# Weight splits of the first mixer ahead in ScalarE's and VectorE's order, and cumulative gate sums in two products

## The chip, the cores and the metric

The kernel runs on one core of one Trainium2 chip. TensorE (PE in the profile) does the matrix products, VectorE (DVE) and ScalarE (ACT) the elementwise work, GpSimd (POOL) some small elementwise work, and SyncE (SP) issues most of the DMAs. Each engine takes its instructions in the order in which they stand in its own queue, and waits by semaphores for what other engines or DMAs have to deliver. The metric is the device time of one execution in microseconds (us); of several executions the median counts.

## The reference

One inference step of a trunk of two layers, for a prompt of 512 tokens and 8 samples of 8 tokens (64 rows), with a model width of 1024. Layer 0 is a forgetting attention in parallel with a gated linear recurrence; layer 1 is a pooling mixer; each is followed by a convolutional feed-forward part. The change touches the first mixer only. Cut to that:

```
def _mixer_ab(xn, past, h0, conv_prev, p, li):
    proj = jnp.einsum("btd,de->bte", xn, p["ab_w_in"][li])
    q, k, v, f, xr, gate = jnp.split(proj, IN_SPLITS, axis=-1)
    q = _rmsnorm(q..., p["ab_q_gain"][li])
    k = _rmsnorm(k..., p["ab_k_gain"][li])
    logf = jax.nn.log_sigmoid(f + p["ab_b_f"][li])
    ...
    c_all = jnp.cumsum(lf_all, axis=1)
    attn = _fox_attention(q, k_all, v_all, c_all[:, past_len:], c_all, ...)
    xc, conv_new = _causal_dwconv(xr, conv_prev, ...)
    h, h_last = _rglru(xc, h0, ...)
    y_rg = h * jax.nn.gelu(gate)
    merged = jnp.concatenate([attn, y_rg], axis=-1)
    out = jnp.einsum("bte,ed->btd", merged, p["ab_w_out"][li])
```

Everything is float32. `logf` has 8 heads; the prompt's 512 tokens lie as 4 chunks of 128 on the partitions, so `cumsum` over tokens is a sum within a chunk plus the totals of the chunks ahead of it.

## The kernel before

The activations stand transposed, features on the partitions, with all 576 tokens in the free dimension. A product in full precision is made of three products in a faster format: each weight and each activation is split into a high part (a cast) and the remainder as low part, and `mm3` (L124 to L137) sums high by high, high by low and low by high, in two column halves of 288 tokens, each into a bank of PSUM. There are 8 banks. `proj_tok` (L550 to L573) does the same with tokens on the output's partitions, four chunks and one bank for the samples.

The weights come from HBM through `raw` (L106 to L111, tile `wraw`, two buffers, DMAs issued by SP). `split` (L112 to L122) makes the high half with a copy on ScalarE (L119) and the low half with a subtraction on VectorE (L120), into the tile `whl`, which has two buffers. So a split can be made at most two ahead of PE's use, and a third waits until PE has read the first.

The order of the instructions on each engine is set by a scheduler when the kernel is built: it takes what is ready by its priority, which follows from the place in the program, unless an instruction is pinned to the program's order or stands in a block that has a high priority. `load_x` is such a block: it transposes x with PE (L346, L347), casts it (L352, L353, and L366, L367 for the samples), and holds the pinned split for the first product `proj(0)` at chunk 5. Its weights, and those of `proj(1)`, lie in one tile, raw0, whose halves are loaded by two DMAs (L329 and L335).

The parts of the mixer, in the program's order: `proj(0)`, the gate product `forget` (L494), the loading and transposing of parameters (`params`: L204 casts the page table into the tile `more`, L206 and L208 transpose parameters), `proj(1)`, then the recurrence's convolutions and gates, the projection of k with `proj_tok`, `branch(0)` (the gate's product, with `gt` L1470), `qk_norm` for k (L595, L596 on ScalarE, L597 to L605 on VectorE), `branch(1)`, the transposes of k (L625 splits, L631 transposes, L633 copies to kT), the recurrence's scan (L1421 to L1433), the projection of q, `branch(2)`, `branch(3)`, the projection of v with background work between its steps, and the output projection `out_proj` over the recurrent half with the evacuation of v (L461 to L463) beside it. In that background stand `sums` (L523 to L538), which makes the prompt's cumulative sums of logf with ten products of 128x8, and `rows` (L545), which transposes them. Attention follows, then the other half of `out_proj`.

Of the kernel before, what the change touches and what calls it, by code (L numbers as in the profile page):

```python
# [2 lines left out]

# [5 lines left out]
F32 = mybir.dt.float32  # L9
# [7 lines left out]
MUL, ADD, SUB = ALU.mult, ALU.add, ALU.subtract  # L17

P = 128
# [7 lines left out]
H = 8  # L27
# [16 lines left out]
class Trunk:  # L44
    def __init__(self, tc, ctx, I, O):
        self.tc, self.nc, self.ctx, self.I, self.O = tc, tc.nc, ctx, I, O
        self.pool = lambda name, **kw: ctx.enter_context(tc.tile_pool(name=name, **kw))
        self.const = self.pool("const", bufs=1)
        self.res = self.pool("res", bufs=1)
        self.wr = self.pool("wr", bufs=2)  # L50
        self.wh = self.pool("wh", bufs=2)
        self.sm = self.pool("sm", bufs=2)
        self.mm = self.pool("mm", bufs=8, space=PSUM)

        self.mid, self.pre, self.bg = deque(), deque(), deque()
        self.up0 = None


    def tick(self):
# [53 lines left out]
    def split(self, v, k, n, pin=False):  # L113

        t = self.wh.tile([P, 2, 1024], F32R, name="whl", tag="whl")
        hi = t[:, 0, 0:k * n].rearrange("p (k n) -> p k n", k=k)
        lo = t[:, 1, 0:k * n].rearrange("p (k n) -> p k n", k=k)
        keep = self.tc.keep_in_program_order if pin else (lambda ins: ins)
        keep(self.nc.scalar.copy(hi, v))  # L119
        keep(self.nc.vector.tensor_tensor(lo, v, hi.bitcast(F32), SUB))  # L120
        return hi, lo

    def mm3(self, whi, wlo, xs, K, first=0):
# [264 lines left out]
    def mixer_ab(self):  # L388
        nc, I, O, tc = self.nc, self.I, self.O, self.tc
        V, A, G, PE = nc.vector, nc.scalar, nc.gpsimd, nc.tensor  # L390
        w_in = I["ab_w_in"][0].rearrange("(k p) n -> p k n", p=P)
        with tc.tile_pool(name="mix", bufs=1, reuse_waits="tile") as mp, ExitStack() as att:
            lf = mp.tile([P, 5, H], F32, name="lf")
# [4 lines left out]
            qn = mp.tile([P, 4, NS], F32, name="qn")  # L398
            kn = mp.tile([P, 4, NS], F32, name="kn")
            bg = self.bg  # L400
            with tc.tile_pool(name="yy", bufs=1, reuse_waits="tile") as yp:
                with tc.tile_pool(name="rg", bufs=1, reuse_waits="tile") as rp:
                    self.tokp = rp
# [73 lines left out]
                self.out_proj(lambda k: (yh[:, k, :], yl[:, k, :]), 4, range(8), prepare)  # L477
            self.attention(mp, aq, q2s, zs, kT, cq, ck, vh, vl, qn, kn, vs, lf, ds, ah, al)
            att.close()
            self.new_xg(1)  # L480
            self.out_proj(lambda k: (ah[:, k, :], al[:, k, :]), 0, (4, 5, 6, 7, 0, 1, 2, 3),
                          lambda m: self.xg_chunk(m, self.g_ffn(0, m)))
# [15 lines left out]
    def gates(self, mp, pf, lf, cq, ck):  # L498


        nc, O = self.nc, self.O
        V, A, G, PE = nc.vector, nc.scalar, nc.gpsimd, nc.tensor
        fT = self.res.tile([16, T], F32, name="fT", tag="sqacc", bufs=1)
        for hf in range(2):
            A.copy(fT[:, hf * HT:(hf + 1) * HT], pf[hf][0:16, 0:HT])

        def logf():
            ft = self.bank()
            for i in range(6):
                a, b, r = (i * P, i * P + P, 0) if i < 4 else (NP, T, (i - 4) * NS)  # L510
                j = min(i, 4) * 16
                PE.matmul(ft[r:r + b - a, j:j + 16], fT[:, a:b], self.ident[0:16, 0:16], start=True, stop=True)
            fsb = self.sm.tile([P, 5, 2, H], F32, name="fsb", tag="fsb", bufs=1)
            A.copy(fsb, ft[:, 0:80].rearrange("p (i a h) -> p i a h", i=5, a=2))
            z = self.sm.tile([P, 5, H], F32, name="z", tag="rs", bufs=1)
            V.tensor_tensor(z, fsb[:, :, 0, :], fsb[:, :, 1, :], ADD)
            V.tensor_tensor(z, z, self.rt.unsqueeze(2).to_broadcast([P, 5, H]), MUL)
            V.tensor_tensor(z, z, self.rowb[:, 128:136].unsqueeze(1).to_broadcast([P, 5, H]), ADD)
            self.logsigmoid(lf.rearrange("p i h -> p (i h)"), z.rearrange("p i h -> p (i h)"), [P, 40], "40")
            nc.sync.dma_start(O["logf_p"][0, 0].rearrange("(i p) h -> p i h", p=P), lf[:, 0:4, :])  # L520
            nc.sync.dma_start(O["logf_s"][0].rearrange("b t h -> (b t) h"), lf[0:NS, 4, :])

        def sums():  # L523
            ct = self.ct = mp.tile([P, 2, 4, 2, 4, 32], F32, name="ct", tag="X")
            pc = self.bank()
            for i in range(4):
                for j in range(i + 1):
                    PE.matmul(pc[:, i * H:(i + 1) * H], self.triu if j == i else self.ones, lf[:, j, :],
                              start=(j == 0), stop=(j == i))
            chi = self.sm.tile([P, 32], F32R, name="chi", tag="chi", bufs=1)  # L530
            V.tensor_copy(chi, pc[:, 0:32])
            G.memset(ct, 0.0)
            G.memset(ct[:, 0, :, :, :, 0:2], 1.0)
            G.memset(ct[:, 1, :, :, :, 2:4], 1.0)
            v4 = lambda t: t.rearrange("p (i t j) -> p i t j", i=4, t=2)
            V.tensor_copy(ct[:, 0, :, :, :, 2], v4(chi.bitcast(F32)))
            V.tensor_tensor(ct[:, 0, :, :, :, 3], v4(pc[:, 0:32]), v4(chi.bitcast(F32)), SUB)
            G.tensor_scalar(ct[:, 1, :, :, :, 0:2], ct[:, 0, :, :, :, 2:4], -1.0, None, MUL)  # L538

        def rows():  # L540
            for a, dst in ((0, cq), (1, ck)):
                for t in range(2):
                    ps = self.bank()
                    for i in range(4):
                        PE.transpose(ps[:, i * P:(i + 1) * P], self.ct[:, a, i, t].rearrange("p j r -> p (j r)"), self.ident)  # L545
                    A.copy(dst[:, t, :], ps)

        self.bg.append(logf)
        return [sums, rows]

    def proj_tok(self, w_in, c0):
# [64 lines left out]
    def k_prep(self, mp, kT):  # L616

        V, A, PE, X = self.nc.vector, self.nc.scalar, self.nc.tensor, self.X
        x2 = mp.tile([P, 2, H, 2, DH], F32R, name="x2", tag="Xq")

        def split(i):
            x = X[:, i, :].rearrange("p (h d) -> p h d", h=H)
            hi, lo = x2[:, i % 2, :, 0, :], x2[:, i % 2, :, 1, :]
            A.copy(hi, x)
            V.tensor_tensor(lo, x, hi.bitcast(F32), SUB)  # L625

        def step(i):
            for a in range(2):
                pt = self.bank()
                for h in range(4):  # L630
                    PE.transpose(pt[:, h * P:(h + 1) * P],  # L631
                                 x2[:, i % 2, 4 * a + h].rearrange("p s d -> p (s d)").bitcast(F32), self.ident)
                (V.tensor_copy if a else A.copy)(kT[:, 4 * a:4 * a + 4, i * P:(i + 1) * P],  # L633
                                                 pt.rearrange("p (h t) -> p h t", h=4))
            if i < 2:
                split(i + 2)

        split(0)
        split(1)
        return [lambda i=i: step(i) for i in range(4)]  # L640
# [878 lines left out]
```

## Time and profile before

| | us |
|---|---|
| median of 3 runs | 1306.14 (1304.78 to 1307.19) |
| the profiled execution | 1310.66 |
| its span | 1308.9 |
| PE busy | 1288.2 (98%) |
| VectorE busy | 813.9 (62%) |
| ScalarE busy | 532.8 (41%) |
| POOL busy | 167.4 (13%) |
| high halves, L119, 176 of them | 183.1 (1.041 each) |
| low halves, L120, 176 of them | 214.7 (1.220 each) |

The span runs from the first to the last instruction; the 1.8 us between it and the execution's own time lie around it. PE is busy nearly throughout, and 20.7 us of the span are not. Busy time says nothing of the pace: PE's clock has two levels, and the page's row of the granted clock, or the windows, show in which of them it worked. The first mixer has 28 of the 176 splits, of which 23 stand ahead of the end of attention and are not pinned; ends of PE's rows are modelled, so a distance between the starts of two rows says more than a duration.

### The profile page before, as it was taken

Reading aid. Unit: us, or ns where it says so; the run is one execution under the profiler, and the core shown is the slowest. Engines: PE = TensorE matmul, PEld = TensorE weight load, DVE = VectorE, ACT = ScalarE, POOL = GpSimd, SP = SyncE. Lnnn points to the kernel's source line nnn. Section 1 sums busy time; section 2 is a strip of 40 time slices with the busy share of each in tenths; the row PEclk is TensorE's granted clock in tenths of the full one; section 3 lists DMA queues with packets and bytes.
Section 4 is the critical chain, followed back from the end, with each engine's and each line's share of the span. In section 5 each row is a group of like instructions: output and inputs, shape, how many; then the busy total and the mean of one; then the engine's idle time right before and its main releaser. Section 6 shows DMA issues by size and latency. Waiting matters only on the chain.

```text
span 1308.9 us, 23023 instructions
## 1 busy us (share of the span) xinstructions
PE 1288.2 (98%) x9462; PEld 1233.3 (94%) x9462; DVE 813.9 (62%) x1559; ACT 532.8 (41%) x877; POOL 167.4 (13%) x527
## 2 busy tenths in 40 slices
PE   8999999999999999999999999999999999999998
PEld 6987888779999999999999999899999999999998
DVE  6847847887767635765367657776743666346742
ACT  6656445674433313332133335444321343124421
POOL 2240053446100000000000002210000000000000
PEclk9999999999999999999999999899999999999999
DMA  6223232424233132312321212232223222223121
GB/s 175 85 67 101 78 130 81 122 60 130 71 100 105 38 97 97 99 65 68 110 83 36 66 50 82 84 131 66 68 67 129 65 82 70 79 97 99 34 92 49
DMA packets 105918, 111.64 MB, mean 85 GB/s; under 512 B 6722, under 2 KB 96970, under 8 KB 105805
## 3 DMA queue, kind: packets, MB, share of 16 engines
q1 hardware_dynamic: 101668, 101.68, 24.2%
q0 software_dynamic: 3072, 8.46, 2.3%
q8 instruction: 74, 1.21, 0.4%
q14 instruction: 32, 0.25, 0.1%
q10 hardware_dynamic: 1072, 0.04, 0.1%
HBM read 104.14 MB, written 6.25 MB: 84 GB/s over the span
## 4 chain that ended last, share of the span: by engine, by line
PE 90%; DVE 5%; ACT 3%; issue 1%; DMA 0%; ACTq 0%
PE mmb L132 77%; PE mmb L564 4%; PE mmb L856 2%; DVE whl L120 1%; PE mmb L821 1%; PE mmb L346 1%; PE mmb L807 1%; DVE xl L282 0%; ACT zh L1098 0%; ACT whl L119 0%; DVE xl L463 0%; PE mmb L494 0%; PE mmb L570 0%; DVE xT L1128 0%; ACT eb L794 0%
## 5 line engine op out<-in xcount | busy, mean ns | idle before, releaser
L132 PE MATMUL mmb<-xh,whl 128*128 128x288 f32 x3456 | 616.5, 298 | 3.3 <-DVE whl L120 1.7
L132 PEld LDWEIGHTS mmb<-xh,whl 128*128 128x128 f32 x3456 | 513.9, 190 | 7.0 <-DVE whl L120 2.2
L132 PE MATMUL mmb<-xl,whl 128*128 128x288 f32 x1728 | 372.6, 297 | 1.6 <-DVE xl L282 1.6
L119 ACT CAST whl<-wraw 128x1024 fp32r<-128x1024 f32 (+1 forms) x176 | 183.1, 1041 | 374.0 <-PE mmb L132 271.6
L132 PEld LDWEIGHTS mmb<-xl,whl 128*128 128x128 f32 x1728 | 280.1, 190 | 2.1 <-DVE xl L282 2.1
L132 PE MATMUL mmb<-hh,whl 128*128 128x288 f32 x1536 | 271.2, 297 | 0.1
L120 DVE TENSOR_TENSOR whl<-wraw,whl 128x1024 fp32r<-128x1024 f32 (+1 forms) x176 | 214.7, 1220 | 79.6 <-ACT whl L119 74.2
L132 PEld LDWEIGHTS mmb<-hh,whl 128*128 128x128 f32 x1536 | 226.2, 188 | 0.7 <-ACT hh L1237 0.6
L132 PE MATMUL mmb<-hl,whl 128*128 128x288 f32 x768 | 165.0, 296 | 0.0
L658 DVE TENSOR_TENSOR xT<-mmb,xT 128x288 f32<-128x288 f32 x128 | 52.6, 452 | 158.9 <-PE mmb L132 158.6
L1217 DVE TENSOR_TENSOR u<-mmb,rb 128x288 f32<-128x288 f32 x96 | 44.0, 458 | 135.4 <-PE mmb L132 127.4
L1222 POOL COPY ut<-u 128x18 f32<-128x18 f32 x96 | 23.1, 241 | 782.3 <-DVE u L1219 782.3
L132 PEld LDWEIGHTS mmb<-hl,whl 128*128 128x128 f32 x768 | 123.1, 188 | 0.0
L1237 ACT CAST hh<-hf 128x576 fp32r<-128x576 f32 x48 | 32.3, 674 | 139.0 <-DVE hf L1234 139.0
L1226 ACT ACTIVATE t<-u,par 128x592 f32<-128x592 f32 x96 | 84.6, 881 | 3.6 <-POOL u L1221 2.0
L1228 DVE SCALAR_TENSOR_TENSOR t<-u,par,t 128x592 f32<-128x592 f32 x96 | 80.1, 835 | 3.4
L1227 DVE SCALAR_TENSOR_TENSOR t<-u,par,t 128x592 f32<-128x592 f32 x96 | 79.6, 830 | 1.1 <-ACT t L1226 1.0
L1231 ACT ACTIVATE t<-t 128x592 f32<-128x592 f32 x48 | 33.6, 699 | 95.0 <-DVE t L1228 95.0
L1238 DVE TENSOR_TENSOR hl<-hf,hh 128x576 fp32r<-128x576 f32 x48 | 36.4, 759 | 34.8 <-ACT hh L1237 34.8
L564 PE MATMUL mmb<-whl,xh 128*128 128x512 f32 x192 | 53.7, 400 | 0.0
L564 PEld LDWEIGHTS mmb<-whl,xh 128*128 128x128 f32 x192 | 35.9, 191 | 8.2
L1218 DVE TENSOR_TENSOR u<-mmb,rb 128x224 f32<-128x224 f32 x96 | 36.6, 382 | 0.0
(383 smaller groups left out, 1311.4 us busy)
## 6 DMA issues: line engine op xcount, KB each, us to landing
wraw<-in_ffn_w_up SPq DMA_DIRECT2D x48, 1024.0 KB
wraw<-in_ffn_w_down SPq DMA_DIRECT2D x24, 1024.0 KB
wraw<-in_ab_w_in SPq DMA_DIRECT2D x9, 1024.0 KB
wraw<-in_ab_w_out SPq DMA_DIRECT2D x4, 1024.0 KB
xt<-in_x_prompt SPq DMA_DIRECT2D x4, 512.0 KB
out_y_p<-y SPq DMA_DIRECT2D x8, 256.0 KB
wraw<-in_ab_w_in SPq DMA_DIRECT2D x2, 512.0 KB
out_k_p<-X SPq DMA_DIRECT2D x1, 1024.0 KB
```

The source lines that it names most:

```text
L119: keep(self.nc.scalar.copy(hi, v))
L120: keep(self.nc.vector.tensor_tensor(lo, v, hi.bitcast(F32), SUB))
L132: nc.tensor.matmul(ps[hf][:, 0:HT], w[:, k, :], x[:, hf * HT:(hf + 1) * HT], start=(n == 0 and j == 0), stop=(n == K - 1 and j == 2))
L564: PE.matmul(ps[i], x[:, i * P:(i + 1) * P], w[:, k2, :], start=(k == 0 and j == 0), stop=(k == 7 and j == 2))
L658: self.nc.vector.tensor_tensor(x, ps[hf][:, 0:HT], x, ADD)
L1217: V.tensor_tensor(u[:, 2:2 + HT], ps[0][:, 0:HT], self.rb[:, 0:HT], MUL)
L1218: V.tensor_tensor(u[:, 2 + HT:514], ps[1][:, 0:NP - HT], self.rb[:, HT:NP], MUL)
L1226: A.activation(t, u[:, 2:594], AF.Identity, scale=self.fw(l, 2, ch), bias=self.fb(l, ch))
L1227: V.scalar_tensor_tensor(t, u[:, 1:593], self.fw(l, 1, ch), t, MUL, ADD)
L1228: V.scalar_tensor_tensor(t, u[:, 0:592], self.fw(l, 0, ch), t, MUL, ADD)
L1231: A.activation(tg[:, 0:592], tg[:, 0:592], AF.Gelu_apprx_tanh)
L1238: V.tensor_tensor(hl, hf_, hh.bitcast(F32), SUB)
```

## The change

A flag `eager` is set when the mixer's body begins, and taken back when attention is done. While it is set, a split that is not pinned is issued in a block of high priority, so that its two instructions go ahead of others that are ready on ScalarE and VectorE. And `sums` forms prefix sums of the chunks on POOL (`pre`) and then needs two products in place of ten: the triangle by all four chunks at once (32 columns), and the ones by the prefixes (24 columns), summed in the same bank.

```
@@ split
-        keep(self.nc.scalar.copy(hi, v))
-        keep(self.nc.vector.tensor_tensor(lo, v, hi.bitcast(F32), SUB))
+        with self.tc.high_priority() if self.eager and not pin else nullcontext():
+            keep(self.nc.scalar.copy(hi, v))
+            keep(self.nc.vector.tensor_tensor(lo, v, hi.bitcast(F32), SUB))
@@ mixer_ab
             bg = self.bg
+            self.eager = True
...
             att.close()
+            self.eager = False
@@ sums
+            pre = self.sm.tile([P, 3, H], F32, name="pre", tag="pre", bufs=1)
+            G.tensor_copy(pre[:, 0], lf[:, 0, :])
+            for i in range(1, 3):
+                G.tensor_tensor(pre[:, i], pre[:, i - 1], lf[:, i, :], ADD)
...
-            for i in range(4):
-                for j in range(i + 1):
-                    PE.matmul(pc[:, i * H:(i + 1) * H], self.triu if j == i else self.ones, lf[:, j, :],
-                              start=(j == 0), stop=(j == i))
+            PE.matmul(pc[:, 0:32], self.triu, lf[:, 0:4, :].rearrange("p i h -> p (i h)"), start=True, stop=False,
+                      skip_group_check=True)
+            PE.matmul(pc[:, 8:32], self.ones, pre.rearrange("p i h -> p (i h)"), start=False, stop=True,
+                      skip_group_check=True)
```

The added lines move the numbers of those behind them by 2, 3, 4, 5 or 10: L119 and L120 become L122 and L123, L204 becomes L207, L1428 becomes L1438.

What stands on VectorE at the start, between the samples' casts of the first half of x (L366, L367) and the cast of the page table (L204). `whl_185` is the split of `proj(0)`. Before:

```order
L367 SCALAR_TENSOR_TENSOR xl_75<-xT_73,gm_78,xh_74 128x64 x2
L353 SCALAR_TENSOR_TENSOR xl_77<-mmb_170,gm_78,xh_76 128x512
L354 COPY xT_73<-mmb_170 128x512
L120 TENSOR_TENSOR whl_185<-wraw_91,whl_185 128x1024
L353 SCALAR_TENSOR_TENSOR xl_77<-mmb_179,gm_78,xh_76 128x512
L353 SCALAR_TENSOR_TENSOR xl_77<-mmb_191,gm_78,xh_76 128x512
```

And now, with `whl_418`, the split of `proj(1)`:

```order
L370 SCALAR_TENSOR_TENSOR xl_75<-xT_73,gm_78,xh_74 128x64
L123 TENSOR_TENSOR whl_418<-wraw_91,whl_418 128x1024
L370 SCALAR_TENSOR_TENSOR xl_75<-xT_73,gm_78,xh_74 128x64
L356 SCALAR_TENSOR_TENSOR xl_77<-mmb_170,gm_78,xh_76 128x512
L357 COPY xT_73<-mmb_170 128x512
L123 TENSOR_TENSOR whl_185<-wraw_91,whl_185 128x1024
L356 SCALAR_TENSOR_TENSOR xl_77<-mmb_179,gm_78,xh_76 128x512
```

The second split's low half moved from far behind (it stood after the first norm's statistics) to ahead of the first split's own. On ScalarE its high half stands directly behind that of `whl_185`, ahead of the copy and casts of chunks 3 and 5 to 7.

VectorE around the recurrence's scans (L1428), where `branch(2)` begins on PE. `whl_1395` and `whl_1457` are the two splits that follow the projection of k. Before:

```order
L1428 SCALAR_TENSOR_TENSOR sq_260<-a__257,xc_258 128x512 x2
L120 TENSOR_TENSOR whl_1395<-wraw_1393,whl_1395 128x1024
L1432 TENSOR_TENSOR sq_260<-a__257,stT_261 128x4x8
L633 CAST kT_245<-mmb_1387 128x4x128
L1433 TENSOR_TENSOR sq_260<-sq_260,xc_258 128x4x8
L120 TENSOR_TENSOR whl_1457<-wraw_1393,whl_1457 128x1024
```

Now, from the last of the scans on (the first three stand ahead of these rows, and `whl_1395` ahead of them all):

```order
L1438 SCALAR_TENSOR_TENSOR sq_260<-a__257,xc_258 128x512
L123 TENSOR_TENSOR whl_1457<-wraw_1393,whl_1457 128x1024
L1438 SCALAR_TENSOR_TENSOR sq_260<-a__257,xc_258 128x512
L643 CAST kT_245<-mmb_1387 128x4x128
L1442 TENSOR_TENSOR sq_260<-a__257,stT_261 128x4x8
```

Both splits moved ahead of scans that they stood behind.

VectorE in the output projection, with L463 for the low part of v, L658 (now L668) for the sums into xT and L725 (now L735) for a part of attention's queries. Before:

```order
L463 TENSOR_TENSOR xl_1829<-vt_1830,xh_1828 128x512
L725 CAST z_1845<-mmb_1846 64x256
L725 CAST z_1854<-mmb_1855 64x256
L120 TENSOR_TENSOR whl_1932<-wraw_1871,whl_1932 128x1024
L658 TENSOR_TENSOR xT_73<-mmb_1904,xT_73 128x288
```

Now (the tile is `whl_1928`):

```order
L123 TENSOR_TENSOR whl_1928<-wraw_1867,whl_1928 128x1024
L732 COPY z_1841<-cq_246 4x128 x2
L732 COPY z_1850<-cq_246 4x128 x2
L467 TENSOR_TENSOR xl_1825<-vt_1826,xh_1824 128x512 x2
L668 TENSOR_TENSOR xT_73<-mmb_1872,xT_73 128x288
```

The low half moved ahead of all four L463 (L467 now).

## Rows read from the trace of the kernel before

**Rows 1.** What PE waited for: us in total, times, longest.

```profile
PE mmb L132 <- DVE whl L120: 3.5, 3, 1.7
...
PE mmb L132 <- ACT whl L119: 0.9, 1, 0.9
...
PE mmb L132 <- ACT kT L633: 0.5, 1, 0.5
```

**Rows 2.** What SP's queue waited for, in the first 120 us.

```profile
SPq L180 <- DMA wraw<-in_ab_w_in: 1.1, 1, 1.1
```

**Rows 3.** Timeline of SP's queue: start, us, instruction.

```profile
13.97 0.22 SPq L180 DMA_DIRECT2D more<-in_ab_q_gain  x1
```

**Rows 4.** Timeline of ScalarE at the start: start, us, instruction, count.

```profile
12.39 1.04 ACT L119 CAST whl<-wraw 128x1024 fp32r<-128x1024 f32 x1
```

**Rows 5.** Timeline of VectorE at the start.

```profile
12.89 0.63 DVE L367 SCALAR_TENSOR_TENSOR xl<-xT,gm,xh 128x64 fp32r<-128x64 f32 x2
13.44 0.74 DVE L353 SCALAR_TENSOR_TENSOR xl<-mmb,gm,xh 128x512 fp32r<-128x512 f32 x1
...
14.70 1.21 DVE L120 TENSOR_TENSOR whl<-wraw,whl 128x1024 fp32r<-128x1024 f32 x1
...
19.99 0.15 DVE L204 CAST more<-more 1x16 f32<-1x16 int32 x1
```

**Rows 6.** Timeline of PE at the start.

```profile
20.35 0.27 PE L206 MATMUL mmb<-ident,more 56*128 56x56 f32 x1
```

**Rows 7.** Timeline of ScalarE at branch(1).

```profile
90.70 1.05 ACT L119 CAST whl<-wraw 128x1024 fp32r<-128x1024 f32 x1
```

**Rows 8.** Timeline of PE at branch(1) and the k heads; in brackets idle time before, releaser.

```profile
91.80 0.53 PE L132 MATMUL mmb<-xh,whl 128*128 128x288 f32 x2 [0.88 <-ACT whl L119]
...
93.15 0.79 PE L132 MATMUL mmb<-xh,whl 128*128 128x288 f32 x4 [0.56 <-DVE whl L120]
...
105.55 1.03 PE L631 MATMUL mmb<-ident,x 128*128 128x128 f32 x8
```

**Rows 9.** Timeline of VectorE at the k heads.

```profile
103.83 1.28 DVE L625 TENSOR_TENSOR x<-X,x 128x512 fp32r<-128x512 f32 x2
```

**Rows 10.** Timeline of VectorE at branch(2).

```profile
129.80 1.20 DVE L120 TENSOR_TENSOR whl<-wraw,whl 128x1024 fp32r<-128x1024 f32 x1
```

**Rows 11.** Timeline of PE at branch(2).

```profile
128.34 0.38 PE L132 MATMUL mmb<-xh,whl 128*128 128x288 f32 x1
...
131.05 1.25 PE L132 MATMUL mmb<-xh,whl 128*128 128x288 f32 x4 [1.19 <-DVE whl L120]
...
135.07 0.69 PE L132 MATMUL mmb<-xh,whl 128*128 128x288 f32 x4
...
135.87 0.70 PE L132 MATMUL mmb<-xh,whl 128*128 128x288 f32 x4
```

**Rows 12.** Timeline of PE at the sums.

```profile
166.19 0.39 PE L528 MATMUL mmb<-lf,triu 128*128 128x8 f32 x2
...
168.45 1.83 PE L564 MATMUL mmb<-whl,xh 128*128 128x512 f32 x4
...
173.34 1.09 PE L564 MATMUL mmb<-whl,xh 128*128 128x512 f32 x4
...
176.57 2.19 PE L545 MATMUL mmb<-ident,ct 128*128 128x128 f32 x16
```

**Rows 13.** Timeline of VectorE at the output projection.

```profile
181.88 4.35 DVE L463 TENSOR_TENSOR xl<-vt,xh 128x512 fp32r<-128x512 f32 x3 [0.64 <-ACT vt L462]
```

**Rows 14.** Timeline of PE at the output projection.

```profile
189.82 0.81 PE L132 MATMUL mmb<-yh,whl 128*128 128x288 f32 x4 [1.72 <-DVE whl L120]
```

**Rows 15.** Windows at branch(2): us, busy by engine, PE's granted clock, DMA share, GB/s.

```profile
130.00:131.00 1.00, 0.00 (x0) 0.00 (x0) 1.00 (x2) 1.00 (x3) 0.98 (x1) 1.00 0.00 0
...
132.00:133.00 1.00, 1.00 (x6) 1.00 (x5) 1.00 (x2) 0.77 (x2) 0.00 (x0) 0.50 0.00 0
```

**Rows 16.** Window behind the sums, columns as in rows 15.

```profile
170.00:171.00 1.00, 1.00 (x4) 0.73 (x3) 0.32 (x1) 0.00 (x0) 0.83 (x2) 0.50 0.03 8
```

More of the change, by code (lines that the diff above doesn't have):

```diff
@@ L1 @@
 from collections import deque
-from contextlib import ExitStack
+from contextlib import ExitStack, nullcontext
 import concourse.bass as bass
@@ L479, in mixer_ab @@
             att.close()
+            self.eager = False
             self.new_xg(1)
```

## The prediction

> **What bounds the kernel now.** I read the table of engines first: TensorE (PE) is busy 98% of the span, so only what PE waits for, or what it executes itself, can move the time. Then the list of PE's waits: in the first mixer it waits three times for the low half of a split weight (VectorE, L120), once for the high half (ScalarE, L119) and once for a kT copy, 4.9 us in all [rows 1]. Outside the start these are all the gaps that the change can close. Then the timelines of ScalarE, VectorE and PE around each gap, to see what the late split stood behind, and last the granted clock in windows of 1 us, since two stretches of the mixer run at half speed. In these stretches PE is not idle in the list and yet loses time. The dumps of the instruction order say what stands where afterwards; all durations are those of the trace.
>
> **The change part by part.** Times are of the profiled execution (1310.66 us, of which the span is 1308.9); a minus is a gain.
>
> *Start, a new wait.* The kernel before does the split for `proj(0)` alone and goes on with the casts of x. Now the split for `proj(1)` (whl_418) stands directly behind it on ScalarE, and its low half stands on VectorE between the two L367 of the first sample half, ahead of the rest of x's preparation. Its raw weights are the second half of raw0. SP's issue of the q gain was held for that transfer [rows 2] and ran at 13.97 [rows 3], so they landed just before 13.97. ScalarE finishes the first split at about 13.4 [rows 4] and now sits until 13.97; the second high half takes 1.04, so it is ready at 15.0. VectorE's low half of 1.21 follows, to 16.2, then the second L367 (half of 0.63), and L353 of chunk 4, which started at 13.44, starts at about 16.4: +3.0 [rows 5]. From there to L204 VectorE has no gap in the trace (20.14 less 13.44 is all work), so L204, the cast of the page table, ends at 23.1 and not at 20.14. PE's L206, a transpose of the tile that L204 writes, follows L204 at once, at 20.35 [rows 6], and everything of PE stands behind it; now it comes at about 23.3. The L494 products ahead of it need no x that is later than they are. After this PE is gapless for 70 us, so the shift stays: **+3.0**. The bounds: +1.1 if only the L120 itself counts (the raw weights are there before ScalarE is free), +4.1 if the transfer lands a further split later. I take the row's 13.97.
>
> *branch(1).* The high half stood behind ten norm activations and ran at 90.70 [rows 7]; PE waited 0.88 for it and 0.56 for the low half [rows 8]. Now it stands behind the first two of the ten, some 4 us earlier, and both waits go. What is late next: in the k norm the low half of the following split now stands ahead of two of the L605, one L120 earlier in VectorE's queue, and with ScalarE's norm activations 0.95 later L625 (103.83, half of a pair) [rows 9] would end at about 105.5 instead of 104.5. PE, freed of 1.44 and of the late starts on either side (about 0.3), and with two L564 now ahead of the L631 that needs it (0.46), would come to that L631 at 104.3 instead of 105.55 and wait 1.2 for it. Of 1.7 some 0.5 is left: **−0.5**, between 0 and −1.7.
>
> *branch(2).* The low half ran at 129.80 behind four scans and four multiplies [rows 10]; now it stands ahead of the first scan, and is done 4 us before PE asks. PE starts this product at 128.34 and gets going at 131.05, four matmuls later; at full pace six take 0.80 (from 135.07 to 135.87), so four take 0.54 [rows 11]. The kT bank wait of 0.5 within it is covered too, as PE now does six matmuls of the other column half first, which is 0.8 us. 2.71 less 0.54 and a remainder of 0.15: **−2.0**; if only the idle part for L120 goes, −1.2.
>
> *Sums.* Ten products are 20 passes, from 166.19 to 168.45: 0.113 each. Two products are four. A pass of 32 columns is not in the trace; between the 8-column pass at 0.113 and the 128-column pass of L545 (2.19 / 16 = 0.137) [rows 12] four cost 0.45 to 0.55: **−1.8**. POOL's copy and two adds come some 100 us ahead of the use, when POOL is idle, and cost nothing; uncovered, they would be under 1 us.
>
> *out_proj.* The low half stood behind three L463 of 4.35 us in all [rows 13] and PE waited 1.72 [rows 14]. Now both halves precede L463. ScalarE's evacuations of ct and v come one split (0.95) later; a bank wait of 0 to 0.5 may follow: **−1.5**, between −1.2 and −1.8.
>
> Other splits of the mixer move as well, and SP's weight loads with them, one of them ahead of the writes of logf. PE's list has no wait for any of these weights after the start, so there is nothing to gain; its lead of several us is what hides them. A loss there would be one split, 1.2.
>
> Sum without clock: 3.0 − 0.5 − 2.0 − 1.8 − 1.5 = **−2.8**.
>
> *Clock.* Behind the window at 130, in which PE is idle, the granted clock is 0.50, that is 1.2 of 2.4 GHz [rows 15]: the 18 L132 from 131.05 to 135.07 take 4.02, where 18 at full pace take 2.4: 1.6 lost [rows 11]. Behind the twenty narrow passes it is 0.50 at 170 [rows 16]: the L564 block from 168.45 to 173.34 takes 4.89, the next, alike, 3.23 to 176.57 [rows 12]: 1.7 lost. Both causes shrink (no gap; four passes in place of twenty), so −3.3 more. Against it stands the new gap at the start. It is 3 us long, where the one at branch(2) was followed by the fall, and those of 1.44 (0.88 and 0.56) [rows 8] and 1.72 [rows 14] were followed by work at full pace. A fall there costs what it cost at 131: +1.6. The three together: −2.8 − 3.3 + 1.6 = **−4.5**.
> The Trainium skill ("TensorE: Matmul & The Clock Gate", Part 1: The HAM clock gate) says that an idle array falls back to 1.2 GHz and regains 2.4 only after being kept busy, which speaks against this change: by it the longest gap, at the start, is the first to be paid for. By that rule alone the sum would be −4.5, without it −6.1; the trace agrees at branch(2) and does not at branch(1) and the output projection.
>
> **How this stands to the median.** The profiled execution is 4.5 us above the median of 1306.14. I carry over the difference, not the level: 1306.14 − 4.5 = 1301.6.
>
> **The rivals.**
> *The clock is not gained.* The half-speed stretches may belong to this one execution (it is 4.5 us slower than the median, and they are worth 3.3), or may come again after four passes as after twenty. For it speaks that gap, against it that both fall on spots that every execution has. Then −2.8, or −1.2 with a fall at the start: 1303.3 to 1304.9.
> *No wait at the start.* If the second half of raw0 is there when ScalarE gets to it and L204's lateness is met by other slack of PE, the term of +3.0 goes: −5.8 without the clock, −9.1 with it: 1297.0 to 1300.3. Against it: the transfer's row is plain.
> *The start decides: slower.* The place is ScalarE's and VectorE's queues at 13 us. The price is the upper bound of 4.1, and a half-speed spell behind a gap of that length that lasts twice as long as the one at 131 and loses 3.3: 7.4. With the other terms at their lower ends (0 at branch(1), 1.2, 1.7 and 1.2: 4.1) and no clock back, the time is 3.3 over the median: 1309.4. It decides from a start of 6.7 (4.1 + 2.6). For it speaks that on VectorE everything up to L204 stands behind the blocked low half; against it that both dearer halves have to come together.
> *Moved, not gained.* The gaps at branch(1), branch(2) and out_proj close, but the next waits of the same chains take their place, as at the L631. Only the sums stay: 3.0 − 1.8 − about 1: 1306 to 1307. What speaks for it is branch(1); against it that at branch(2) nothing waits behind the split but small scans.
>
> **How the numbers follow.** Forecast 0.45, with 1299.5 to 1303.5 as its own range; clock not gained 0.20; no wait at the start 0.12; start decides 0.12; moved 0.11. A measurement of this kernel tells some 0.2%, 2.6 us, from no change, that is outside 1303.5 to 1308.8. Faster: 0.42 + 0.05 + 0.12 = 0.59. Same: 0.03 + 0.15 + 0.09 + 0.02 = 0.29. Slower: 0.10 + 0.02 = 0.12. The range 1298.0 to 1307.5 leaves out the lower half of "no wait" and most of "start decides", under 0.2.
>
> **What would show it.** In the profile after: PE's list with a wait of about 3 us for L204 (now L207) and none of over 0.5 for the mixer's L119 and L120 (now L122, L123); ScalarE idle for half a us between two splits at 13.5; a wait of PE at the transposes of the first k heads near 105; four passes in place of twenty, with the clock at 1.00 behind them; and the clock at 1.00 where `branch(2)` begins. A start without the wait, or a clock of 0.50 that stays behind the sums, would make the forecast wrong.

## The result

The kernel after takes 1296.39 us (median of 4 runs, 1295.60 to 1297.09), the kernel before 1306.42 (1304.78 to 1307.19): a ratio of 0.9923 [0.9911, 0.9936], 10.0 us less. The forecast was 1301.6 with a range of 1298.0 to 1307.5. The sign was right; the gain, 0.8%, is more than twice the forecast 4.5, and the time lies below the range. The profiled execution of after took 1295.6 us (span 1293.9, granted clock 0.997).

PE's list of waits in the kernel after: of what stood in [rows 1] nothing is left, and one short bank wait is new.

```profile
PE mmb L343 <- DMA gr<-in_norm_mix: 3.5, 1, 3.5
PE mmb L349 <- DMA xt<-in_x_prompt: 1.7, 1, 1.7
PE mmb L817 <- DVE st L805: 1.4, 1, 1.4
PE mmb L135 <- DVE xl L285: 1.1, 2, 0.8
...
PE mmb L555 <- DVE both L588: 0.3, 1, 0.3
```

The wait that the forecast put at the start is missing: no L209 and nothing on L207.

**Start.** ScalarE's timeline after, start, us and instruction (answers to [rows 4]):

```profile
14.08 1.05 ACT L122 CAST whl<-wraw 128x1024 fp32r<-128x1024 f32 x1 [0.47 <-DMA wraw<-in_ab_w_in]
```

VectorE's (to [rows 5]):

```profile
15.16 1.23 DVE L123 TENSOR_TENSOR whl<-wraw,whl 128x1024 fp32r<-128x1024 f32 x1 [1.80 <-ACT whl L122]
16.50 0.74 DVE L356 SCALAR_TENSOR_TENSOR xl<-mmb,gm,xh 128x512 fp32r<-128x512 f32 x1
...
23.05 0.15 DVE L207 CAST more<-more 1x16 f32<-1x16 int32 x1
```

PE's (to [rows 6]):

```profile
21.27 0.27 PE L209 MATMUL mmb<-ident,more 56*128 56x56 f32 x1
...
29.50 0.52 PE L214 MATMUL mmb<-more,ones 1*128 1x152 f32 x2
```

Up to VectorE all came as worked out: ScalarE sits 0.47 for the raw weights, chunk 4 starts at 16.50 (forecast 16.4), the cast of the page table ends at 23.20 (forecast 23.1). But PE's transpose L209 runs at 21.27, ahead of that cast. It does not wait for it.

**branch(1) and the k heads.** ScalarE, VectorE and PE after (to [rows 7 to 9]):

```profile
85.46 1.04 ACT L122 CAST whl<-wraw 128x1024 fp32r<-128x1024 f32 x1
```
```profile
104.33 1.27 DVE L635 TENSOR_TENSOR x<-X,x 128x512 fp32r<-128x512 f32 x2
```
```profile
104.44 0.63 PE L574 MATMUL mmb<-whl,xh 128*128 128x512 f32 x2
105.06 1.09 PE L641 MATMUL mmb<-ident,x 128*128 128x128 f32 x8
```

Both waits are gone. The wait of 1.2 that was to come behind the first k heads is not in the list.

**branch(2).** VectorE, PE and the window behind it, after (to [rows 10, 11, 15]); a window's columns are us, busy share of PE, PEld, VectorE, ScalarE and POOL, granted clock, DMA share, GB/s:

```profile
123.19 1.22 DVE L123 TENSOR_TENSOR whl<-wraw,whl 128x1024 fp32r<-128x1024 f32 x1
```
```profile
127.31 0.38 PE L135 MATMUL mmb<-xh,whl 128*128 128x288 f32 x1
127.65 0.43 PE L135 MATMUL mmb<-xh,whl 128*128 128x288 f32 x2
```
```profile
130.00:131.00 1.00, 1.00 (x10) 1.00 (x9) 1.00 (x2) 1.00 (x2) 0.00 (x0) 1.00 0.00 0
```

The low half is done 3 us before PE asks; no gap, and no spell at 1.2 GHz behind it.

**Sums and output projection.** PE after, and the window behind the sums (to [rows 12, 14, 16]):

```profile
161.52 0.41 PE L536 MATMUL mmb<-lf,triu 128*128 128x32 f32 x2
161.77 0.38 PE L538 MATMUL mmb<-pre,ones 128*128 128x24 f32 x2
161.99 1.18 PE L574 MATMUL mmb<-whl,xh 128*128 128x512 f32 x4
...
170.22 0.63 PE L555 MATMUL mmb<-ident,ct 128*128 128x128 f32 x4 [0.28 <-DVE both L588]
...
179.98 0.69 PE L135 MATMUL mmb<-yh,whl 128*128 128x288 f32 x4
180.51 0.42 PE L135 MATMUL mmb<-yl,whl 128*128 128x288 f32 x2
```
```profile
163.00:164.00 1.00, 1.00 (x6) 0.83 (x5) 0.88 (x1) 0.00 (x0) 1.00 (x1) 1.00 0.00 0
```

Four passes take 161.52 to 161.99, 0.47; the clock stays at 1.00 behind them. The product that waited 1.72 follows without a gap.

**Where the time went, by stages of PE.** Each stage runs from the start of one marked instruction in PE's timeline to the start of the next (us). The first mark is the transpose L206 (L209 after); what lies ahead of it is not in the table, and it starts at 20.35, 20.98, 21.27 and 19.99 us in the four profiles. Two profiles of each kernel, since a second one of before, taken with the experiments (1305.9 us, span 1304.2), differs from the first in four stages although the program is the same.

| stage | before | before, again | after | after, again |
|---|---|---|---|---|
| L206 to the end of the k projection | 63.79 | 63.81 | 63.74 | 63.79 |
| branch(1) | 17.95 | 16.48 | 16.00 | 15.99 |
| q projection | 25.23 | 25.22 | 25.28 | 25.28 |
| branch(2) | 11.30 | 9.77 | 7.79 | 7.79 |
| next products | 27.18 | 27.18 | 27.05 | 27.06 |
| sums and the block behind | 10.77 | 10.74 | 7.34 | 7.33 |
| up to q's transposes | 3.99 | 3.99 | 4.19 | 4.19 |
| output projection | 28.03 | 28.03 | 25.68 | 25.88 |
| attention | 118.61 | 117.77 | 116.53 | 116.55 |
| the rest | 977.22 | 975.70 | 974.44 | 974.53 |

Between the two middle profiles, which lie nearest to the medians (before again, after): 0.5 at branch(1), 2.0 at branch(2), 3.4 at the sums, 2.15 at the output projection (2.35 less the 0.20 of the new bank wait ahead of it; 1.95 by the second profile of after), and 1.2 each in the attention and the rest, where the order did not change.

### The profile page after: what moved, and what is told of

It reads as the page before. It is cut to its first block, busy times and chain, and to the rows that moved or that the text cites. A ratio compares the mean times of both kernels' runs of the same rounds, so it can differ in the third digit from the quotient of the medians.

```text
span 1293.9 us, 23002 instructions
## 1 busy us (share of the span) xinstructions
PE 1278.9 (99%) x9446; PEld 1226.2 (95%) x9446; DVE 813.7 (63%) x1559; ACT 532.0 (41%) x877; POOL 168.5 (13%) x530
## 4 chain that ended last, share of the span: by engine, by line
PE 94%; DVE 3%; ACT 2%; issue 1%; DMA 0%; ACTq 0%
PE mmb L135 78%; PE mmb L574 5%; PE mmb L866 2%; PE mmb L1098 1%; PE mmb L831 1%; PE mmb L349 1%; PE mmb L817 0%; DVE xl L285 0%; PE mmb L499 0%; PE mmb L580 0%; PE mmb L578 0%; DVE whl L123 0%; PE mmb L883 0%; DMA xt<-in_x_prompt 0%; PE mmb L1191 0%
## 5 line engine op out<-in xcount | busy, mean ns | idle before, releaser
L122 ACT CAST whl<-wraw 128x1024 fp32r<-128x1024 f32 (+1 forms) x176 | 182.9, 1040 | 369.9 <-PE mmb L135 269.7
L123 DVE TENSOR_TENSOR whl<-wraw,whl 128x1024 fp32r<-128x1024 f32 (+1 forms) x176 | 214.6, 1220 | 82.5 <-ACT whl L122 82.1
L668 DVE TENSOR_TENSOR xT<-mmb,xT 128x288 f32<-128x288 f32 x128 | 52.6, 452 | 157.0 <-PE mmb L135 156.8
L1232 POOL COPY ut<-u 128x18 f32<-128x18 f32 x96 | 23.1, 241 | 776.4 <-DVE u L1229 776.4
L574 PE MATMUL mmb<-whl,xh 128*128 128x512 f32 x192 | 53.2, 394 | 0.0
L574 PEld LDWEIGHTS mmb<-whl,xh 128*128 128x128 f32 x192 | 35.4, 188 | 8.1 <-ACT a__257 L1421 0.3
```

What stands on the lines that cost most here:

```text
L574: PE.matmul(ps[i], x[:, i * P:(i + 1) * P], w[:, k2, :], start=(k == 0 and j == 0), stop=(k == 7 and j == 2))
L668: self.nc.vector.tensor_tensor(x, ps[hf][:, 0:HT], x, ADD)
```

## The experiments

**1. Is there a wait at the start?** Theory A (the forecast): L206 needs what L204 writes, and the delay of VectorE costs 3 us. Theory B: it needs something else, and the delay costs nothing. First the kernel before with priority for that one split alone:

```diff
+                    self.eager = True
                     rg.proj(1)
+                    self.eager = False
```

> The kernel before, with the high priority for the split of proj(1) alone. Theory A (L206 never waited for L204, whose row only stood beside it): VectorE is 3 us late at the start and PE does not see it; 1306.4, between -0.5 and +1. Theory B (the prediction: PE's L206 waits for L204): PE waits 3 us and the kernel takes 1309.4. Theory C (the late start of the full clock seen in the changed kernel comes from this move): +0.9, 1307.3, with L494 at half pace until 20.3 us.

Then the kernel after without that split's priority:

```diff
-            self.eager = True
...
                     rg.proj(1)
+                    self.eager = True
```

> The changed kernel, with the split of proj(1) back at its ordinary place (the flag is set after proj(1)). Theory A (the early split at the start costs nothing): the same as the changed kernel, 1296.4 within 1. Theory B (it costs what it adds to VectorE): 3 us less, 1293.4. Theory C (it costs a later start of the full clock): 0.9 less, 1295.5.

Measured: 0.9996 [0.9985, 1.0007] and 0.9922 [0.9906, 0.9938] to before; the kernel after has 0.9923. So no cost of the start is to be seen, with the rest of the change or without it: alone it is a gain of 0.5 us, between a loss of 0.9 and a gain of 2.0, and a loss of 3 lies outside. VectorE and PE of the first kernel:

```profile
15.50 1.23 DVE L123 TENSOR_TENSOR whl<-wraw,whl 128x1024 fp32r<-128x1024 f32 x1 [2.23 <-ACT whl L122]
...
23.39 0.15 DVE L207 CAST more<-more 1x16 f32<-1x16 int32 x1
```
```profile
20.90 0.27 PE L209 MATMUL mmb<-ident,more 56*128 56x56 f32 x1
```

The cast is 3.4 us later than in [rows 5], the transpose only 0.55 later than in [rows 6], and 2.5 ahead of the cast. The code says why: L207 writes `more[0:1, 264:280]`, L209 reads `more[0:56, 0:P]`, columns 0 to 127. Same tile, other columns, no dependence. The reader of the cast is L214, which reads `more[0:1, 128:280]` and runs at 29.50 in the kernel after, 6.3 us behind the cast's end. That is the cover. The 0.55 is not the split's either: over all thirteen profiles this instruction starts anywhere from 18.50 to 23.09, on average at 21.18 in the five with the split ahead and at 21.12 in the eight without. In all five it starts ahead of the cast, by 1.7 to 4.2 us. VectorE's lateness does reach PE in one of them, the second profile of after, in which PE's clock was at 2.4 GHz from 13 us on and PE came to the L494 products (L499 there) early:

```profile
18.47 0.30 PE L499 MATMUL mmb<-xl,wf 128*16 128x288 f32 x1 [0.25 <-DVE xl L356]
```

It is a wait for a cast of x, not for the page table, and a quarter of a us; the forecast had none at these products. The unchanged kernel run again, with 20.98, had the expectation:

> The kernel before, unchanged, for a second profile. If the two stretches at half speed (behind the gap at branch(2) and behind the sums) belong to the kernel, the granted clock is 0.50 there again, and the 18 L132 and the L564 block take 4.0 and 4.9 us again. If they belonged to the one profiled execution (which was 4.5 us above the median), one or both run at full pace, and the profiled time is nearer to 1306.

**2. Which part gives the rest?** The new sums alone on the kernel before, run twice, on two chips, and the priority alone, on a third chip (the kernel after with the ten products of before in the place of the two):

```diff
+            PE.matmul(pc[:, 0:32], self.triu, lf[:, 0:4, :]...
+            PE.matmul(pc[:, 8:32], self.ones, pre...
-            for i in range(4):
-                for j in range(i + 1):
...
```

> The kernel before, with the two products and the prefix sums alone. Theory A (passes and the half-speed stretch behind them both go): -1.8 and -1.7, so -3.5 us, 1302.9. Rival (the half-speed stretch is not in the timed executions): -1.8, 1304.6. Second rival (the stretch stays behind four passes too): -1.8 as well, but with a clock of 0.50 in the profile behind them.

> The two sums alone once more, on the chip of the two others of this call. Theory A: -3.4 (two products and no half-speed stretch), 0.9974. Rival (the stretch is in few of the timed executions): -1.8, 0.9986. What the changed kernel has beyond this is the worth of the early splits: 4.6 by the places with an undisturbed branch(1), 6 with a late one.

> The changed kernel with the old sums of ten products, so the priority of the splits alone. Theory A (the places add up as PE's markers in a usual execution have them: start 0.2, branch(1) -0.5, branch(2) -2.0, output projection -1.9): -4.2, 1302.3. Theory B (the whole move less the sums alone): 10.0 - 4.5 = -5.6, 1300.9. Prediction as it stood: +3.0 - 0.5 - 2.0 - 1.5 = -1.0 and up to +1.6 of clock, 1305.4 to 1307.0. In the profile the half-speed stretch stays behind the ten narrow products.

Measured: 0.9967 [0.9956, 0.9979] and 0.9959 [0.9945, 0.9972] for the sums (4.3 and 5.4 us), 0.9975 [0.9961, 0.9989] for the priority (3.3). The stage of the sums falls from 10.74 to 7.34 with the two products in all five profiles that have them. With the ten it is 10.73 to 10.77 in five profiles (the kernel before twice, the start, branch(1) and branch(2) alone) and 9.17 in two (the priority alone, and the output projection alone), where no spell follows (a spell is a stretch in which the granted clock is 0.50, that is 1.2 GHz). PE and the window, priority alone:

```profile
168.25 0.39 PE L533 MATMUL mmb<-lf,triu 128*128 128x8 f32 x2
...
170.50 1.18 PE L569 MATMUL mmb<-whl,xh 128*128 128x512 f32 x4
```
```profile
171.00:172.00 1.00, 1.00 (x6) 0.79 (x6) 1.00 (x3) 0.00 (x0) 0.64 (x1) 1.00 0.00 0
```

The same twenty passes as in [rows 12] (2.25 here, 2.26 there), and the block behind them takes 1.18 at 2.4 GHz where it took 1.83. So 1.83 of the sums' 3.4 is the passes (9.17 less 7.34), which is there always; 1.6 is a spell at 1.2 GHz that followed the ten products in 5 of 7 profiles. The two profiles without it are also the only two of the seven in which the splits of the output projection stand ahead; no run tells whether that order decides or something else.

The profile of the priority alone also holds a wait of PE of 2.8 us in the k projection (put down to "issue": nothing that the profile shows), which no profile of before or after has:

```profile
83.76 0.50 PE L1413 MATMUL mmb<-xch,wb 128*128 128x300 f32 x1 [2.84 <-issue]
```

With a spell behind it the stage up to the end of the k projection takes 68.50 there, 4.7 more than in the table. The 3.3 may be short by some of it; how many of the timed executions have the wait is not known.

**3. Do the narrow passes bring the spell?** The kernel after with eight products of 8 columns into unused columns of the bank, so 20 passes again (with them the kernel's results are not those of the reference; only its time is of use):

```diff
+            for i in range(8):
+                PE.matmul(pc[:, 64 + i * H:72 + i * H], self.ones, lf[:, i % 4, :], start=True, stop=True,
+                          skip_group_check=True)
```

> The changed kernel, with eight more products of 128x8 (16 passes) between its two sums, into unused columns of the same bank, so twenty passes as before. Their results are not used. Theory A (narrow passes in a row bring the half-speed stretch): 16 passes of 0.113 are 1.8, and the stretch behind them costs 1.7 more: 1299.9, with the clock at 0.50 behind them in the profile. Rival (the stretch came from where the old products stood in time, not from their number): +1.8 alone, 1298.2, at full clock.

Measured: 0.9963 [0.9951, 0.9975], and in the profile, PE and the window behind:

```profile
163.62 1.93 PE L539 MATMUL mmb<-lf,ones 128*128 128x8 f32 x16
165.40 0.38 PE L541 MATMUL mmb<-pre,ones 128*128 128x24 f32 x2
165.63 1.18 PE L577 MATMUL mmb<-whl,xh 128*128 128x512 f32 x4
```
```profile
166.00:167.00 1.00, 1.00 (x6) 0.82 (x5) 0.91 (x4) 0.00 (x0) 0.50 (x1) 1.00 0.00 0
```

The sixteen passes cost 1.8 (the stage is 9.12 against 7.34), 0.11 each, as the forecast had it; in this one profile no spell follows. This misses what the theory of the spell expected. But the spell was missing behind the old ten in 2 of 7 too, in kernels with the output projection's splits ahead, as they are here, so one profile can't refute it. That narrow passes bring the spell is not shown, nor that they do not. By the ratios the kernel lies 5 us over the kernel after, more than 1.8, but the two were not timed on one chip; its profile has a wait of 2.3 us in the k projection like the one above and a spell at 288 us. Inconclusive beyond the price of the passes.

**4. The three gaps, one at a time.** Kernel before, with priority around one call each:

```diff
+                    self.eager = True
                     rg.branch(1)
+                    self.eager = False
```

> The kernel before, with the high priority for the split of branch(1) alone. PE's stretch from the end of the projection of k to the end of the next product behind branch(1) was 16.5 us in three profiles with the late split and 17.9 in three others (there ScalarE's norm began 1.3 us later), and 16.0 in the changed kernel. Theory A (the timed executions are like the 16.5): -0.5 us. Theory B (like the 17.9): -1.9. In the profile of this kernel the stretch is 16.0 and PE does not wait at the transposes of the first k heads, as the following split is not early here.

The same around `rg.branch(2)`:

> The kernel before, with the high priority for the split of branch(2) alone. Theory A (only the gap goes): -2.0, 1304.4. Theory B (the half-speed stretch behind the gap is in the timed executions as in the first profile): -3.6, 1302.8. In the profile VectorE's low half stands ahead of the first scan and PE has no wait of 1.2 us there.

And around the first `self.out_proj(...)`:

> The kernel before, with the high priority for the four splits of the recurrent half of the output projection alone. Theory A (the wait of 1.72 goes, nothing takes its place): -1.8, 1304.6. Rival (ScalarE's evacuations, one split later, hold a bank of PE): -1.2 or less, with a new wait of PE of 0.5 at the transposes of ct.

Measured: 0.9992 [0.9983, 1.0001], 0.9983 [0.9971, 0.9996] and 0.9977 [0.9962, 0.9991], that is 1.0 (from a loss of 0.1 to 2.2), 2.2 (0.5 to 3.8) and 3.0 us (1.2 to 5.0). These intervals do not tell the theories of branch(1) and branch(2) apart; the stages of the profiles do. By stages: branch(1) 16.01; branch(2) 7.69; output projection 28.03 to 25.88, with 0.19 given back at the new bank wait. The profile of branch(1) alone shows the spell behind the untouched gap at branch(2), its second window at half clock:

```profile
130.00:131.00 1.00, 0.18 (x1) 0.18 (x2) 1.00 (x3) 1.00 (x3) 0.92 (x1) 0.98 0.03 8
131.00:132.00 1.00, 1.00 (x5) 1.00 (x6) 1.00 (x3) 1.00 (x3) 0.00 (x0) 0.50 0.00 0
```

The kernel before, run again, has the same gap and no spell, PE and a window:

```profile
130.21 0.80 PE L132 MATMUL mmb<-xh,whl 128*128 128x288 f32 x4 [1.17 <-DVE whl L120]
```
```profile
167.00:168.00 1.00, 1.00 (x4) 0.71 (x4) 0.96 (x1) 0.00 (x0) 1.00 (x1) 0.50 0.00 0
```

Its four matmuls take 0.80 where [rows 11] have 1.25; the second window is the one behind the sums, where the spell is there as in [rows 16]. Of the seven profiles with the gap at branch(2), two have the spell behind it, one of the two of the unchanged kernel among them.

branch(1) differs among executions in another way. ScalarE and PE of the kernel before in the profile that the forecast used:

```profile
84.89 0.69 ACT L595 ACTIVATE X<-mmb,rt 128x512 f32<-128x512 f32 x1 [5.79 <-PE mmb L570]
```
```profile
84.14 0.39 PE L570 MATMUL mmb<-whl,xsl 128*64 128x512 f32 x1
```

and run again:

```profile
84.07 0.69 ACT L595 ACTIVATE X<-mmb,rt 128x512 f32<-128x512 f32 x1 [4.33 <-PE mmb L564]
```
```profile
84.79 0.39 PE L570 MATMUL mmb<-whl,xsl 128*64 128x512 f32 x1
...
92.32 0.79 PE L132 MATMUL mmb<-xh,whl 128*128 128x288 f32 x4 [0.22 <-DVE whl L120]
```

In the first, ScalarE's norm starts 0.75 behind the start of PE's L570, in the second 0.72 ahead of it; everything on ScalarE, the split of branch(1) among it, is as much later in the first, and PE's gap is 1.44 there and 0.22 here. Of seven profiles with the split in its old place, three have the late norm (stage 17.87 to 17.95) and four the early one (16.47 to 16.48). With the split ahead of the norm all six have 15.99 to 16.01. The runs give a place for it: the four kernels of experiments 2 to 4 that were timed on one chip (the priority, branch(2) and the output projection alone, and the kernel of experiment 3) had before at 1309.9 us beside them, where the two other chips had it at 1306.5 and 1306.7. Of the profiles taken there the two with the split in its old place have the late norm. All four also take 74.5 to 75.4 us in the attention from its first L856 to its last L719, where every other profile takes 72.7 to 72.9, save one: the first profile of before, with a late norm and 74.5, whose chip is not known. 1.5 at the norm and 1.8 there come near the 3.4 between the chips. So the late norm goes with a chip and not with single executions, as far as these profiles show. Why it does so stays open.

**5. The kernel after, again.**

> The changed kernel once more, beside the two others of this call, to see whether the parts add up on one chip. Theory A (they add up): the ratio 0.992 again, 10 us less than before, and the profile's mixer as in the first profile. Rival (the first ratio was high by chance; the places sum to 7 to 8): 0.994.

Measured: 0.9923 [0.9910, 0.9937], 1296.15 us; its stages are in the table. On this chip the sums alone gave 5.4 of the 10.1, which leaves 4.7 for the splits, and the places give 4.6 (0.5, 2.0 and 2.15). None of the kernels run beats it: the one of experiment 1 without the start's split equals it (0.9922).

## Why the prediction was wrong

**The step that failed: "PE's L206, a transpose of the tile that L204 writes, follows L204 at once".** It was read from two neighbouring rows (19.99 plus 0.15, then 20.35) and from the tile's name. The rows were neighbours by chance: the transpose reads other columns of the tile. The term of +3.0 is 0 as far as the runs can tell, and with it goes the +1.6 for a fall of the clock behind that gap: 4.6 of the 5.5 us between the forecast gain of 4.5 and the measured 10.0. Without the two the sum is −9.1, which is the rival "no wait at the start" at its lower end, 1297.0; the gain by the ratio's interval is 8.4 to 11.6. That rival was put down to the transfer or to slack of PE, not to the dependence itself, which two lines of the code would have settled. The replay of ScalarE and VectorE up to that step was right to 0.1 us in the first profile of after; in the second the moved low half starts 1.2 later still, which was the forecast's upper bound, and PE does not wait for the cast there either. Nothing is known from this on the Trainium skill's rule that an idle array falls back to 1.2 GHz ("TensorE: Matmul & The Clock Gate", Part 1: The HAM clock gate) at the start, since there was no gap; at branch(2) a gap of 1.17 to 1.31 with one of 0.5 just before it was followed by the fall in 2 of 7 profiles, so a forecast from that gap needs a chance beside the price.

**Terms that were mis-sized.**
- branch(1): forecast −0.5 as 1.7 less a new wait of 1.2. Measured −0.49 from an execution with an early norm and −1.95 from one with a late one; timed alone −1.0 [−2.2, +0.1]. The new wait of 1.2 did not come (the transposes at 105.06 follow the L574 of 104.44 without an entry in the list), since its working took over the lateness of ScalarE from an execution in which it was late. Counted from the start of the last L570 of the k projection (L580 after), the subtractions that split k (L625, L635 after) start at 18.2 us in before run again, at 19.3 after and at 19.7 in the profile that the forecast used [rows 9]. The 1.0 that the moved split adds is there (1.1), but on top of the early norm, and PE, at its transposes 20.05 behind that mark, finds the first of the pair done. That −0.5 was met is luck: the gap of 1.7 and the wait of 1.2 both came from the late norm.
- branch(2): forecast −2.0, measured −1.98, alone −2.08 (9.77 to 7.69). Right. Its clock term of −1.6 was real in the profile that it was read from and in one other of seven; over the seven it comes to some −0.4 (1.53 times 2 of 7, which is few to take a chance from).
- Sums: forecast −1.8 for the passes, measured −1.83; clock forecast −1.7, measured −1.6 where there was a spell, in all five profiles that have the ten products with the output projection's splits in their old places. Right. That two products brought none in five of five profiles was the part of the forecast that the rival "the clock is not gained" denied.
- Output projection: forecast −1.5, between −1.2 and −1.8. Measured −2.15 to −2.35, and 0.2 back at the bank wait that the forecast allowed 0 to 0.5 (behind ScalarE, it said; the profile names VectorE's L588). The gap of 1.72 went whole; what else went is not taken apart.

**What the forecast did not have.** Some 2.5 us in the attention and the rest, whose instructions stand in the same order.

In the rest 1.1 us comes with the new sums. From the second L1181 of the second layer (L1191 after) to the last PE instruction, PE takes 451.58 or 451.59 us in all seven profiles with the ten products and 450.43 to 450.45 in all six with the two. First and last row in before run again and in after:

```profile
848.09 0.27 PE L1181 MATMUL mmb<-ident,fst 64*128 64x64 f32 x1
1299.67 0.27 PE L1284 MATMUL mmb<-ident,xT 128*64 128x128 f32 x1
```
```profile
838.89 0.27 PE L1191 MATMUL mmb<-ident,fst 64*128 64x64 f32 x1
1289.31 0.27 PE L1294 MATMUL mmb<-ident,xT 128*64 128x128 f32 x1
```

The priority alone has 451.58 and the kernel with the sixteen passes put back 450.43, so it is neither the splits nor the number of passes. It builds up in small steps, none over 0.04 us; why the new sums quicken PE so far behind them is not shown. With it the sums are worth 3.4 + 1.1 = 4.5, near the 4.3 and 5.4 that they gave when timed alone.

In the attention it is, for the kernel before run again, a spell at 1.2 GHz from 289 to 292 us that neither profile of after has:

```profile
289.00:292.00 3.00, 3.00 (x16) 3.00 (x14) 1.78 (x7) 1.15 (x4) 2.83 (x15) 0.50 1.01 336
```

But the first profile of before has none there either, and of the experiments some have it (the start, branch(1), the priority and the sums alone, both times, and experiment 3, at 287 to 295) and some not (branch(2) and the output projection alone, and the kernel after without the start's split). Whether the change takes it away, or these profiles fell that way, no run here settles.

**The level.** The difference was carried over from a profile 4.5 us above the median as if it held for the median. By the table that profile stands above the second one by 1.5 at branch(1), 1.5 at branch(2), 0.8 in the attention and 1.5 in the rest: two of the terms were read in the very stages in which it was unusual. The 1.5 in the rest is a spell from 834 to 841 us (granted clock 0.52 over these 7 us), twice as long as the one in the second profile, from 832 to 835. This cost little only by luck: the clock term of 1.6 at branch(2), which five of the seven profiles do not have, stands against the 2.5 us that the forecast did not have.

## What to carry to other kernels

Before two neighbouring rows are taken for a wait, look in the code whether the region that the one reads overlaps the region that the other writes; a tile's name is not a region, and the instruction that does read it sets the slack. A late start, a gap's size or a spell at half clock that one profile shows is priced only when a second profile of the same program, on another chip if there is one, shows it again; else it is a term with a chance. A split that is moved far ahead of its use pays off twice: its gap goes, and PE no longer follows every lateness of the engine that it was queued on (branch(1): 16.47 to 17.95 before, 15.99 to 16.01 after).

## What the runs showed of the hardware

- A pass of an f32 product with 32 or 24 columns costs about what one with 8 does: four in 0.47 us (0.118 each), against twenty of 8 columns in 2.26 (0.113 each). What counts at these sizes is the number of passes.
- Spells at 1.2 GHz do not belong to a spot of the program. Behind the gap of 1.2 to 1.3 at branch(2) PE went on at full clock in five profiles and at half in two, of the unchanged kernel once each. Behind the ten products it was at half in five and at full in two, but these two are other programs than the five.
- At the start PE's L494 products come 0.24 us apart and then 0.13 apart. The change comes at a time that differs from run to run in both orders: from 18.4 us in the kernel of experiment 3 to 22.5 with the priority alone, and in two profiles (after again, and the output projection alone) they come 0.13 apart from the first, at 16 to 17 us, but for the short wait told of in experiment 1.
- One program's time differed by 3.4 us between chips (1306.5, 1306.7 and 1309.9 us for the kernel before).
